# A decoder trunk of two layers on one core: the attention gates as rows made by one product of ones, with bias and partial sums on VectorE

## The chip, the cores and the metric

One core of one Trainium2 chip. The time is the device time of one execution, in microseconds (us); a version's time is the median of its runs.

## The reference, cut to what matters

One sequence of 256 tokens, width 1024, runs through two layers; each is a token mixer and then a mixture of experts (MoE). Layer 0 mixes with stick-breaking attention (16 heads of 64), layer 1 with retention (8 heads, projections 1024 to 6144 and 2048 to 1024). All four sub-layers are modulated by a conditioning vector c:

```python
def adaln_params(c, w, b):
    m = jax.nn.silu(c) @ w + b            # w: 1024 x 3072
    shift, scale, gate = jnp.split(m, 3, axis=-1)
...
for i in range(DEPTH):
    shift, scale, gate = adaln_params(c, ada_w[i, 0], ada_b[i, 0])
    h = x * (1.0 + scale) + shift
    y = stick_breaking_attention(h, ...) if i % 2 == 0 else retention(h, ...)
    x = layer_norm(DEEPNORM_ALPHA * x + (1.0 + gate) * y, ln_g[i, 0], ln_b[i, 0])
    shift, scale, gate = adaln_params(c, ada_w[i, 1], ada_b[i, 1])
    y = grouped_moe(x * (1.0 + scale) + shift, ...)      # 16 experts, top 2
    x = layer_norm(DEEPNORM_ALPHA * x + (1.0 + gate) * y, ln_g[i, 1], ln_b[i, 1])
```

The vector `1 + gate` of the two token mixers is what the change is about.

## The kernel before

The stages follow one another: the stick-breaking attention (called STICK), the MoE of layer 0, retention (RETEN), the MoE of layer 1. In the traces they begin near 40, 180, 445 and 610 us. Within a stage a tile framework orders every engine's instructions by a simulated timeline, so a change in the Python code reorders the work around it. All loads are issued by SyncE (SP) in one queue, 1 MB each.

**Dense blocks.** A weight arrives as fp32. `split_to` makes two parts of it: ScalarE copies a rounded high part (L382), VectorE subtracts to get the low part (L383). `mm3` then runs three matmuls for each product (L403, L404, L405). The token mixers consist mostly of these.

**Stick-breaking attention** works in two halves of 8 heads, `stick_in` and then `stick_attn`. `stick_in` makes q, k and v by dense blocks; v is copied out of PSUM by VectorE (L603). `stick_attn` goes over 4 pairs of heads: the score product z on TensorE (L615, L617), the causal addition on VectorE (L619), three activations on ScalarE (L621 to L623), a combination on VectorE (L624), the suffix sums px on TensorE (L627, L628), their addition on VectorE (L629), an exponential on ScalarE (L630), the product with v on TensorE (L634, L635). z and px have one PSUM buffer each, so the next pair's z waits until VectorE has read the last one, and px likewise.

**The modulation vectors** are computed in the gaps. Sub-layer i (0 attention, 1 its MoE, 2 retention, 3 its MoE) has six chunks j of 512 columns: 0, 1 shift, 2, 3 scale, 4, 5 gate. `plan` puts (i, j) on a list, and each `fill()` between dense blocks takes the next chunk (`ada_part`) and finishes the one before (`rest`). A chunk's weights come in two 1 MB loads. On VectorE it is eight operations, L280 for the first and L282 for seven more, each weight row block times one entry of silu(c) per partition, summed into the tile `e` (128x512). With `on_pe=True` TensorE does it in 16 short matmuls (L277). `rest` then takes the column sums of `e` in four products with `ones` that come out transposed (L292), VectorE adds the bias (L293) and, for scale and gate, 1 (L296). The gate is wanted as a row, equal on all partitions: `gate_row` turns the sums back by four matmuls with the identity for each half (L235) and ScalarE copies each half out (L358). Its tile has one buffer. Chunks (0,4), (0,5) and (2,5) run on VectorE, (2,4) on TensorE.

**Around the change.** The gate of layer 0 is wanted by `out_proj` after the second attention half, that of layer 1 by `ret_out` after the last dense block of retention. `fill` calls stand in `stick_in` after q, after k and after v, and in retention after its dense blocks.

## Time and profile before

| | |
|---|---|
| runs | 904.66, 906.91, 908.5 us; median 906.91 |
| profiled execution | 906.52 us, of which the instructions span 904.8 |
| TensorE busy | 846.6 us (94% of the span) |
| VectorE busy | 499.5 us (55%) |
| ScalarE busy | 274.6 us (30%) |
| GpSimd busy | 21.9 us (2%) |
| DMA | 310.05 MB, mean 343 GB/s |
| mean granted TensorE clock | 0.969 of full speed |

A busy share is an average over four stages with different limits; it doesn't say which engine a given stage waits for. PE stands for TensorE, DVE for VectorE, ACT for ScalarE, POOL for GpSimd, SP for SyncE.

### The profile page before, as it was taken

Reading aid. Unit: us, or ns where it says so; the run is one execution under the profiler, and the core shown is the slowest. Engines: PE = TensorE matmul, PEld = TensorE weight load, DVE = VectorE, ACT = ScalarE, POOL = GpSimd, SP = SyncE. Lnnn points to the kernel's source line nnn. Section 1 sums busy time; section 2 is a strip of 40 time slices with the busy share of each in tenths; the row PEclk is TensorE's granted clock in tenths of the full one; section 3 lists DMA queues with packets and bytes.
Section 4 is the critical chain, followed back from the end, with each engine's and each line's share of the span. In section 5 each row is a group of like instructions: output and inputs, shape, how many; then the busy total and the mean of one; then the engine's idle time right before and its main releaser. Section 6 shows DMA issues by size and latency. Waiting matters only on the chain. (4 is left out here: it accounts for less than half of the span.)

```text
span 904.8 us, 11162 instructions
## 1 busy us (share of the span) xinstructions
PE 846.6 (94%) x4345; PEld 515.9 (57%) x4345; DVE 499.5 (55%) x943; ACT 274.6 (30%) x387; POOL 21.9 (2%) x44
## 2 busy tenths in 40 slices
PE   5799999989969999999799999999999999999993
PEld 1497887764424443434578888888853434334432
DVE  0389999836232235242797899848755423332225
ACT  1347656143101011100534545646341101101101
POOL 0000000000000000000000120011000000000000
PEclk8799999989989999999999999999989999999997
DMA  8999989797999999999679877929749999999971
GB/s 300 386 386 386 365 317 374 265 375 276 420 414 411 416 421 415 416 416 388 210 230 358 310 262 271 332 84 366 291 173 401 416 415 418 415 417 417 418 308 46
DMA packets 90035, 310.05 MB, mean 343 GB/s; under 512 B 5652, under 2 KB 6092, under 8 KB 73588
## 3 DMA queue, kind: packets, MB, share of 16 engines
q1 hardware_dynamic: 89972, 309.23, 88.5%
q8 instruction: 37, 0.61, 0.3%
q14 instruction: 26, 0.21, 0.1%
HBM read 308.17 MB, written 1.05 MB: 342 GB/s over the span
## 5 line engine op out<-in xcount | busy, mean ns | idle before, releaser
L969 PE MATMUL ps<-s,xg 128*64 128x512 f32 x632 | 168.3, 600 | 2.2 <-DVEq L862 1.4
L969 PE MATMUL ps<-w,xg 128*64 128x512 f32 x392 | 111.9, 606 | 6.3 <-PEq L862 6.3
L969 PEld LDWEIGHTS ps<-s,xg 128*64 128x64 f32 x632 | 53.2, 138 | 88.1 <-issue 82.8
L1086 PE MATMUL ps<-w,hidT 128*64 128x512 f32 (+1 forms) x296 | 83.6, 574 | 0.1
L382 ACT ACTIVATE wp<-w 128x1024 fp32r<-128x1024 f32 x57 | 60.1, 1058 | 67.2 <-PE ps L405 60.7
L383 DVE TENSOR_TENSOR wp<-w,wp 128x1024 fp32r<-128x1024 f32 x57 | 69.4, 1220 | 15.1 <-ACT wp L382 14.9
L1019 DVE TENSOR_TENSOR mosg<-mosg,ps 128x512 f32<-128x512 f32 x16 | 11.0, 688 | 118.0 <-PE ps L969 118.0
L1086 PE MATMUL ps<-s,hidT 128*64 128x512 f32 (+1 forms) x248 | 71.8, 568 | 0.0
L969 PEld LDWEIGHTS ps<-w,xg 128*64 128x64 f32 x392 | 35.5, 139 | 63.1 <-issue 60.8
L282 DVE SCALAR_TENSOR_TENSOR s<-w,cact,s 128x512 f32<-128x512 f32 x88 | 65.7, 746 | 0.7
L1051 DVE SCALAR_TENSOR_TENSOR moy<-ps,cs,gate 128x512 f32<-128x512 f32 (+1 forms) x34 | 24.3, 716 | 71.8 <-PE ps L1086 71.8
L382 ACT ACTIVATE moyh<-moy 128x512 fp32r<-128x512 f32 (+1 forms) x34 | 20.6, 605 | 124.2 <-DVE moy L1051 124.2
L404 PE MATMUL ps<-wp,hh 128*128 128x512 f32 (+1 forms) x144 | 56.4, 394 | 0.0
L405 PE MATMUL ps<-wp,hl 128*128 128x512 f32 x144 | 55.5, 390 | 0.0
L454 ACT ACTIVATE xg<-ps,mod 128x256 f32<-128x256 f32 x32 | 17.8, 564 | 122.3 <-PE ps L940 122.3
L403 PE MATMUL ps<-wp,hh 128*128 128x512 f32 (+1 forms) x144 | 53.4, 393 | 1.3 <-ACT wp L382 0.7
L1067 DVE TENSOR_TENSOR res<-res,ps 128x512 f32<-128x512 f32 x48 | 30.3, 683 | 36.7 <-PE ps L1062 36.3
L1086 PEld LDWEIGHTS ps<-w,hidT 128*64 128x64 f32 x296 | 27.1, 136 | 34.0 <-issue 30.9
L1017 ACT ACTIVATE mosg<-ps 128x512 f32<-128x512 f32 x16 | 9.5, 597 | 110.6 <-PE ps L969 110.6
L1086 PEld LDWEIGHTS ps<-s,hidT 128*64 128x64 f32 x248 | 24.7, 137 | 29.9 <-issue 28.8
L403 PE MATMUL ps<-s,wp 128*128 128x256 f32 x128 | 36.6, 288 | 0.6 <-DVE fcol L222 0.6
L405 PE MATMUL ps<-s,wp 128*128 128x256 f32 x128 | 35.2, 285 | 1.1 <-DVE wp L383 1.1
(342 smaller groups left out, 1503.2 us busy)
## 6 DMA issues: line engine op xcount, KB each, us to landing
s<-in_moe_w_up SPq DMA_DIRECT2D x45, 1024.0 KB, 14.5
w<-in_ada_w SPq DMA_DIRECT2D x39, 1024.0 KB, 8.0
w<-in_moe_w_down SPq DMA_DIRECT2D x35, 1024.0 KB, 15.1
s<-in_moe_w_gate SPq DMA_DIRECT2D x34, 1024.0 KB, 13.2
w<-in_moe_w_gate SPq DMA_DIRECT2D x30, 1024.0 KB, 15.3
s<-in_moe_w_down SPq DMA_DIRECT2D x29, 1024.0 KB, 18.2
w<-in_moe_w_up SPq DMA_DIRECT2D x19, 1024.0 KB, 18.5
w<-in_ret_w_in SPq DMA_DIRECT2D x18, 1024.0 KB, 7.1
```

The lines of the kernel that those rows point to most:

```text
L282: V.scalar_tensor_tensor(e, wt[:, kk, :], cact[:, k:k + 1], e, op0=OP.mult, op1=OP.add)
L382: A.activation(hi, src, AF.Copy)
L383: return V.tensor_tensor(lo, src, hi, op=OP.subtract).ins
L403: T.matmul(dst, lh, rh, start=start, stop=False)
L404: T.matmul(dst, lh, rl, start=False, stop=False)
L405: state["mm"] = T.matmul(dst, ll, rh, start=False, stop=stop).ins
L454: return A.activation(dst, src, AF.Identity, scale=sc[:, k:k + 1], bias=sh[:, k:k + 1]).ins
L969: state["mm"] = T.matmul(o[64 * u:64 * u + 64, :], xg[:, k, at:at + CAP], ts[u][kk], start=(k == 0), stop=(k == NK - 1)).ins
L1019: V.tensor_tensor(sgt, sgt, pu, op=OP.mult)
L1051: V.scalar_tensor_tensor(y, py, cs, gate[:, c0:c0 + n], op0=OP.mult, op1=OP.mult)
L1067: V.tensor_tensor(r, r, sos[b], op=OP.add)
L1086: state["mm"] = T.matmul(py[64 * u:64 * u + 64, :], hidT[:, f, u * CAP:(u + 1) * CAP], ts[h][u][:, i, c0:c0 + n], start=(f == 0), stop=(f ...
```

## The change

The chunks (0,4), (0,5), (2,4) and (2,5), the gates of the two token mixers, become `direct`. A zeroed tile `brow` (128x512, one buffer, kept for the whole program) takes the chunk's bias row in its first partition by a DMA of 2 KB; the first of the eight VectorE operations adds `brow` instead of only multiplying (L287 of the changed kernel); the finishing step `row` is one product of the 128x128 tile `ones` with `e`, which sums over the partitions and leaves the sum on all of them at once, and one ScalarE copy that adds 1 and writes half of the gate row. `rest` and `gate_row` go for these chunks. Chunk (2,4) moves from TensorE to VectorE. The MoE gates keep `rest` and `gate_row`.

```diff
+    sums, gates = {}, {}
+    brow = keep([P, 512], "brow")
+    G.memset(brow, 0.0)
...
+        direct = i % 2 == 0 and j >= 4
+        if direct:
+            if i not in gates:
+                gates[i] = tmp([P, D], "gate", 1)
+            SY.dma_start(brow[0:1, :], ada_b[l, s, j * 512:(j + 1) * 512].rearrange("(o d) -> o d", o=1))
...
+                elif k == 0 and direct:
+                    V.scalar_tensor_tensor(e, wt[:, kk, :], cact[:, 0:1], brow, op0=OP.mult, op1=OP.add)
...
+        def row():
+            pt = ps((P, 512), "po" if state["name"] == "RETEN" else "ps")
+            T.matmul(pt, ones, e, start=True, stop=True)
+            A.activation(gates[i][:, (j - 4) * 512:(j - 3) * 512], pt, AF.Copy, bias=1.0)
...
-        return rest
+        return row if direct else rest
...
-        gate = gate_row(2)
+        gate = gates[2]
...
-    gate = gate_row(0)
+    gate = gates[0]
...
-    plan(2, range(4, 5), on_pe=True)
-    plan(2, range(5, 6))
+    plan(2, range(4, 6))
```

Lines of the old code stand 7 to 15 lines further down in the changed kernel: L282 is L291 there, L383 L398, L403 to L405 L418 to L420, L603 L618, L615 L630, L619 L634, L624 L639, L627 and L628 L642 and L643, L629 L644. New are L278 (DMA of the bias row), L287 (first operation of a direct chunk), L301 (product with ones), L302 (copy of the row).

TensorE, first attention half, before: px of a pair of heads, then dense products (names `ps`, with weights `wp`), then z of the next pair, then the next dense block.

```order
L627 MATMUL px_620<-s_135 128x384
L628 MATMUL px_620<-s_135 128x128
L627 MATMUL px_620<-s_135 128x384
L628 MATMUL px_620<-s_135 128x128
L404 MATMUL ps_520<-wp_571,s_200 128x512
...
L615 MATMUL pz_658<-s_251,s_252 128x256 x2
L617 MATMUL pz_658<-s_251,s_252 128x128 x2
L403 MATMUL ps_707<-s_200,wp_711 128x256
L404 MATMUL ps_707<-s_201,wp_711 128x256
```

The same place in the changed kernel:

```order
L420 MATMUL ps_522<-wp_572,s_203 128x512
L630 MATMUL pz_655<-s_253,s_254 128x256 x2
L632 MATMUL pz_655<-s_253,s_254 128x128 x2
L642 MATMUL px_617<-s_137 128x384
L643 MATMUL px_617<-s_137 128x128
L642 MATMUL px_617<-s_137 128x384
L643 MATMUL px_617<-s_137 128x128
L630 MATMUL pz_679<-s_253,s_254 128x256 x2
L632 MATMUL pz_679<-s_253,s_254 128x128 x2
L642 MATMUL px_641<-s_82,s_137 128x384
L643 MATMUL px_641<-s_82,s_137 128x128
L642 MATMUL px_641<-s_82,s_137 128x384
```

Four attention steps stand back to back, with no dense product between them. Behind them follow the products with v, the row product L301 of chunk (0,5) and only then the dense block that stood between them.

VectorE at the same place, before. L282 are the operations of the modulation chunks, L383 splits of dense weights, L603 the copies of v.

```order
L383 TENSOR_TENSOR wp_711<-lo_709,wp_711 128x1024
L629 TENSOR_TENSOR s_207<-s_207,px_620 128x768
L280 TENSOR_SCALAR s_82<-w_831,cact 128x512
L603 COPY s_252<-ps_520 128x512
L282 SCALAR_TENSOR_TENSOR s_82<-w_831,cact,s_82 128x512
L603 COPY s_252<-ps_521 128x512
L282 SCALAR_TENSOR_TENSOR s_82<-w_831,cact,s_82 128x512
L619 TENSOR_TENSOR s_207<-pz_658,s_135 128x768
L383 TENSOR_TENSOR wp_738<-lo_709,wp_738 128x1024
L282 SCALAR_TENSOR_TENSOR s_82<-w_831,cact,s_82 128x512
L624 SCALAR_TENSOR_TENSOR s_82<-s_82 128x768
```

The changed kernel:

```order
L398 TENSOR_TENSOR wp_708<-lo_706,wp_708 128x1024
L618 COPY s_254<-ps_521 128x512
L291 SCALAR_TENSOR_TENSOR s_82<-lo_599,cact,s_82 128x512
L618 COPY s_254<-ps_522 128x512
L291 SCALAR_TENSOR_TENSOR s_137<-w_515,cact,s_137 128x512
L398 TENSOR_TENSOR wp_735<-lo_706,wp_735 128x1024
L634 TENSOR_TENSOR s_209<-pz_655,s_137 128x768
L639 SCALAR_TENSOR_TENSOR s_82<-s_82 128x768
L291 SCALAR_TENSOR_TENSOR s_82<-lo_599,cact,s_82 128x512
L644 TENSOR_TENSOR s_209<-s_209,px_617 128x768
L291 SCALAR_TENSOR_TENSOR s_137<-w_515,cact,s_137 128x512
L634 TENSOR_TENSOR s_137<-pz_679,s_137 128x768
```

The third causal addition (L619, now L634) stands behind the split and both copies in either; the addition of the suffix sums (L629, now L644), which stood ahead of the copies, now stands behind the third causal addition and the combination L639.

VectorE in the first dense blocks of retention, before. L645 to L651 are the rotary embedding.

```order
L383 TENSOR_TENSOR s_3343<-w_3341,s_3343 128x1024
L383 TENSOR_TENSOR wp_3358<-w_3341,wp_3358 128x1024
L383 TENSOR_TENSOR wp_3387<-w_3385,wp_3387 128x1024
L383 TENSOR_TENSOR s_3402<-w_3385,s_3402 128x1024
L645 TENSOR_TENSOR s_3373<-ps_3307,trig 128x512
L649 TENSOR_TENSOR s_3374<-ps_3307,trig 128x4x64 x2
L645 TENSOR_TENSOR s_3373<-ps_3308,trig 128x512
L649 TENSOR_TENSOR s_3374<-ps_3308,trig 128x4x64 x2
L651 TENSOR_TENSOR s_3373<-s_3373,s_3374 128x512
L383 TENSOR_TENSOR wp_3419<-w_3417,wp_3419 128x1024
```

The changed kernel, with chunk (2,4) now on VectorE:

```order
L398 TENSOR_TENSOR s_3327<-w_3325,s_3327 128x1024
L398 TENSOR_TENSOR wp_3342<-w_3325,wp_3342 128x1024
L287 SCALAR_TENSOR_TENSOR s_3257<-w_3544,cact,brow 128x512
L398 TENSOR_TENSOR wp_3371<-w_3369,wp_3371 128x1024
L291 SCALAR_TENSOR_TENSOR s_3257<-w_3544,cact,s_3257 128x512
L398 TENSOR_TENSOR s_3386<-w_3369,s_3386 128x1024
L291 SCALAR_TENSOR_TENSOR s_3257<-w_3544,cact,s_3257 128x512
L660 TENSOR_TENSOR s_3357<-ps_3291,trig 128x512
L664 TENSOR_TENSOR s_3358<-ps_3291,trig 128x4x64 x2
L660 TENSOR_TENSOR s_3357<-ps_3292,trig 128x512
L664 TENSOR_TENSOR s_3358<-ps_3292,trig 128x4x64 x2
L291 SCALAR_TENSOR_TENSOR s_3257<-w_3544,cact,s_3257 128x512
```

Operations of chunk (2,4) stand between the splits (L398) from the fourth one on; before, the first operation of a gate chunk stood behind the place shown.

## Rows read from the trace of the kernel before

**Rows 1.** The chain of work that ended last, followed back from the last instruction: shares of the span by engine.

```profile
PE 17%; DVE 2%; ACT 0%; issue 0%; DVEq 0%; ACTq 0%
```

**Rows 2.** Five stretches of 20 us, one in each stage (two in retention): length, then busy time (and count) of PE, PE's weight loads, DVE, ACT, POOL; then the granted clock, the DMA share, GB/s.

```profile
140.00:160.00 20.00, 19.80 (x112) 14.96 (x111) 18.48 (x29) 12.62 (x19) 0.00 (x0) 1.00 0.99 377
200.00:220.00 20.00, 18.45 (x99) 8.60 (x99) 12.51 (x25) 6.33 (x9) 0.00 (x0) 1.00 0.58 217
460.00:480.00 20.00, 20.00 (x102) 15.23 (x101) 19.16 (x29) 8.70 (x11) 0.00 (x0) 1.00 0.81 275
560.00:580.00 20.00, 20.00 (x105) 16.95 (x104) 19.96 (x37) 12.24 (x20) 0.00 (x0) 1.00 0.98 345
700.00:720.00 20.00, 20.00 (x102) 8.71 (x98) 7.20 (x13) 2.28 (x4) 0.00 (x0) 1.00 1.01 415
```

**Rows 3.** ScalarE's longest wait from 440 to 540 us: what waited, what for; us in total, times, longest.

```profile
ACT wp L382 <- PE ps L405: 28.7, 17, 5.1
```

**Rows 4.** TensorE in order of time, for prices (here and in all groups below: start, duration, engine, line, operation, tiles, form, count): the four transposing products of a chunk (fp32, two instructions each) and the product behind them, half of `gate_row` (four products, likewise) and the product behind it, two pairs of 256 columns in fp32, the 16 products of chunk (2,4) and the product behind them.

```profile
177.12 0.95 PE L292 MATMUL ps<-con,s 128*128 128x2 f32 x8
178.01 0.64 PE L277 MATMUL ps<-lo,cact 128*32 128x512 f32 x4
...
143.54 1.16 PE L235 MATMUL ps<-con,sums 128*128 128x128 f32 x8
144.45 0.47 PE L403 MATMUL ps<-wp,oh 128*128 128x512 f32 x1
...
607.23 0.59 PE L690 MATMUL pz<-s,s 128*128 128x256 f32 x2
607.66 0.59 PE L691 MATMUL pz<-s,s 128*128 128x256 f32 x2
...
471.05 1.92 PE L277 MATMUL ps<-w,cact 128*32 128x512 f32 x16
472.90 0.50 PE L403 MATMUL ps<-wp,hh 128*128 128x512 f32 x1
473.24 0.40 PE L404 MATMUL ps<-wp,hh 128*128 128x512 f32 x1
```

**Rows 5.** TensorE in the first attention half: px of a pair and the product behind it, z of the next pair and the product behind it, a product with v and the product behind it.

```profile
78.41 0.81 PE L627 MATMUL px<-s 128*128 128x384 f32 x2
...
80.06 0.48 PE L404 MATMUL ps<-wp,s 128*128 128x512 f32 x1
...
82.53 0.70 PE L615 MATMUL pz<-s,s 64*128 64x256 f32 x4
...
83.38 0.38 PE L403 MATMUL ps<-s,wp 128*128 128x256 f32 x1
...
99.35 0.66 PE L634 MATMUL po<-s,s 128*64 128x256 f32 x4
...
100.16 0.39 PE L403 MATMUL ps<-s,wp 128*128 128x256 f32 x1
```

**Rows 6.** VectorE in the first attention half, three places.

```profile
70.37 0.95 DVE L619 TENSOR_TENSOR s<-pz,s 128x768 f32<-128x768 f32 x1
71.24 0.74 DVE L282 SCALAR_TENSOR_TENSOR s<-w,cact,s 128x512 f32<-128x512 f32 x1
71.90 1.22 DVE L383 TENSOR_TENSOR wp<-w,wp 128x1024 fp32r<-128x1024 f32 x1
73.03 0.15 DVE L293 TENSOR_TENSOR sums<-ps,col 128x4 f32<-128x4 f32 x1
73.11 0.74 DVE L282 SCALAR_TENSOR_TENSOR s<-lo,cact,s 128x512 f32<-128x512 f32 x1
...
83.01 0.48 DVE L280 TENSOR_SCALAR s<-w,cact 128x512 f32<-128x512 f32 x1
83.41 0.68 DVE L603 COPY s<-ps 128x512 f32<-128x512 f32 x1
84.01 0.74 DVE L282 SCALAR_TENSOR_TENSOR s<-w,cact,s 128x512 f32<-128x512 f32 x1
...
93.12 0.95 DVE L624 SCALAR_TENSOR_TENSOR s<-s 128x768 f32<-128x768 f32 x1
93.98 0.74 DVE L282 SCALAR_TENSOR_TENSOR s<-w,cact,s 128x512 f32<-128x512 f32 x1
```

**Rows 7.** TensorE in the output projection of the attention; in square brackets the idle time before the instruction and what ended it.

```profile
168.56 0.50 PE L404 MATMUL ps<-wp,oh 128*128 128x512 f32 x1 [0.94 <-DVE wp L383]
```

**Rows 8.** VectorE in retention, splits of dense weights and one operation of a modulation chunk.

```profile
452.24 1.23 DVE L383 TENSOR_TENSOR s<-w,s 128x1024 fp32r<-128x1024 f32 x1 [1.67 <-ACT s L382]
...
470.05 1.22 DVE L383 TENSOR_TENSOR wp<-w,wp 128x1024 fp32r<-128x1024 f32 x1
471.19 0.75 DVE L282 SCALAR_TENSOR_TENSOR s<-w,cact,s 128x512 f32<-128x512 f32 x1
...
476.84 1.23 DVE L383 TENSOR_TENSOR wp<-lo,wp 128x1024 fp32r<-128x1024 f32 x1 [0.77 <-ACT wp L382]
...
482.98 1.23 DVE L383 TENSOR_TENSOR wp<-lo,wp 128x1024 fp32r<-128x1024 f32 x1 [0.81 <-ACT wp L382]
485.69 1.23 DVE L383 TENSOR_TENSOR wp<-w,wp 128x1024 fp32r<-128x1024 f32 x1 [1.49 <-ACT wp L382]
...
489.62 1.23 DVE L383 TENSOR_TENSOR s<-w,s 128x1024 fp32r<-128x1024 f32 x1 [2.31 <-ACT s L382]
```

**Rows 9.** SyncE's issue of the load that stands behind the second bias row in the changed kernel; and loads by destination and source with the median us from issue to landing.

```profile
55.19 2.50 SPq L165 DMA_DIRECT2D s<-in_sb_w_in  x1
...
lo<-in_ada_w SPq DMA_DIRECT2D x6, 1024.0 KB, 10.6
...
w<-in_sb_w_in SPq DMA_DIRECT2D x8, 1024.0 KB, 14.5
...
w<-in_moe_w_up SPq DMA_DIRECT2D x19, 1024.0 KB, 18.5
```

**Rows 10.** ScalarE in the first attention half: the load of an activation table and the activation behind it.

```profile
72.48 1.28 ACT L622 ACT_TABLE_LOAD   x1
73.77 0.84 ACT L622 ACTIVATE s<-s 128x768 f32<-128x768 f32 x1
```

More of the change, by code (lines that the diff above doesn't have):

```diff
@@ L261, in rotary_tables @@
             V.tensor_scalar(trig[:, 1, b, :], trig[:, 2, b, :], -1.0, None, op0=OP.mult)
-    sums = {}
+    sums, gates = {}, {}
+    brow = keep([P, 512], "brow")
+    G.memset(brow, 0.0)
     def ada_part(i, j, on_pe):
```

## The prediction

> **What bounds the kernel now.** I read the chain of waits first, and it answers little here: it follows the end of the program back through the last MoE only (17% of the span on TensorE) [rows 1]. So I went to the stretches by stage [rows 2]. The reader is to see two kinds. In the attention of layer 0 and in retention TensorE is busy 19.80 and 20.00 of 20 us, and VectorE stands right beside it, at 18.48, 19.16 and 19.96 of 20. In the MoE of layer 1 the DMA moves 415 GB/s at a share of 1.01, with VectorE at 7.20. Between the two lies the start of the first MoE: there the DMA share is 0.58, so the loads wait for buffers that TensorE has to free, and a shift of the attention's end is passed on. The waits of ScalarE say the same for retention: its splits waited 28.7 us for products (L405) that had to free their buffers, 17 times [rows 3]. Both attention stages run at TensorE's pace, with a VectorE that has almost nothing to spare; the granted clock is 1.00 in all five stretches, so the sum needs no term for it.
>
> I therefore count TensorE's work in the two stages, and look for each place where the new order makes it wait for VectorE. A microsecond there is a microsecond at the end. The sum is made against the profiled execution, 906.52 us, 0.4 below the median of the runs shown (906.91).
>
> **TensorE's work in the attention of layer 0.** Durations are taken from one start to the next, since products overlap. The four transposing products of a chunk take 0.95 as their row gives it (0.89 from start to start; I keep the row's), half of `gate_row` 144.45 − 143.54 = 0.91 [rows 4]. The new row product, 512 columns in fp32, has no row of its own; the nearest are two fp32 pairs of 256 columns, 607.66 − 607.23 = 0.43 each, so 0.86. Its bounds are 0.43 (one pass of the two would do) and 0.95 (no better than what it replaces); 0.86 is the same form and length. Two chunks: −2 x 0.95 − 2 x 0.91 + 2 x 0.86 = **−2.0 us**.
>
> **The order in the first half.** Before, the four attention steps stand between dense products. After, z, px, z, px, the products with v and the row product of chunk (0,5) stand back to back behind the last dense product. z and px have one PSUM buffer each, so every step of this run needs VectorE to have read the one before. Without any wait the next dense block would begin at 83.38 (as before) − 0.95 (products that go) + 1.65 (px, 80.06 − 78.41) + 0.85 (z, 83.38 − 82.53) + 0.81 (product with v, 100.16 − 99.35) + 0.86 = 86.6 [rows 5].
>
> Against this stands what VectorE has to do first. Its steps, from start to start: causal addition 0.87, modulation product 0.66, split 1.13, copy of v 0.60, combination 0.86 [rows 6]. In the new order, from the first causal addition at 70.37 to the end of the third (which frees z for the fourth pair) there stand 3 x 0.87 + 9 x 0.66 + 4 x 1.13 + 0.86 + 2 x 0.60 = 15.13 us, so the fourth z begins at 85.5 at the earliest. The second px needs VectorE's first suffix addition: 0.86 + 0.66 + 0.86 later, 87.9. The row product needs the last two products of its chunk, behind the next causal addition: 0.66 + 0.87 + 2 x 0.66 later, 90.7. With 0.86 for itself the dense block begins at 91.6 in place of 86.6: **+5.0 us**. Bounds: nothing, if VectorE's work ahead of 70.37 comes earlier by as much; 5.0 is taken because VectorE is 90% busy here and nothing is taken off it.
>
> **The order in the second half** is like it: the third z, px, the fourth z, px and the products with v, without the dense products that stood between the two px. From the end of the dense products VectorE has a copy, a product, a copy, the combination, a split and a causal addition ahead of the fourth z: 0.60 + 0.66 + 0.60 + 0.86 + 1.13 + 0.87, and twice the 0.08 of a small addition (73.11 − 73.03) [rows 6], 4.9 us. TensorE has 0.85 + 1.65 = 2.5. That is +2.4; the suffix addition then ends at 4.9 + 0.66 + 0.86 = 6.4 where TensorE is at 5.75: +0.65. Together **+3.0 us**.
>
> In the output projection TensorE now waits 0.94 for a split [rows 7]; a TensorE that comes later by more than that finds it done: **−0.9**. The stage: −2.0 + 5.0 + 3.0 − 0.9 = **+5.1 us**.
>
> **Retention.** TensorE is rid of the 16 products of chunk (2,4), 472.90 − 471.05 = 1.85, of two times four transposing products (−1.9) and of `gate_row` (−1.8), and gets two row products (+1.7): **−3.85 us**. VectorE gets eight products, 8 x 0.66 = 5.3. Six more than before stand ahead of the split at 470.05, 4.0 us; VectorE was idle for 1.67 before the split at 452.24 and fills that, so this split ends 2.3 later, at 473.6. TensorE wanted it at 473.24 and wants it at 471.4 without the 16 products [rows 4, 8]: **+2.2 us**. Behind it VectorE has 0.77, 0.81, 1.49 and 2.31 idle ahead of its next splits [rows 8], which take up the rest. The stage: −3.85 + 2.2 = **−1.65 us**.
>
> **What I cost at nothing.** Clearing `brow` is GpSimd's, idle in all stretches [rows 2]. The bias in the first product makes it a operation with two inputs, 0.66 in place of 0.40 (83.41 − 83.01) [rows 6], in three chunks, counted at 0.66 above; against that go L293 and L296 of four chunks. The copy of the row replaces that of `gate_row` one to one on ScalarE. `brow` has one buffer: each next bias row waits on SP's queue for the first product of the chunk before, and with it every load behind it; by the order on VectorE that product stands a whole chunk earlier, so I add nothing, and price the other case below. ScalarE loads its activation tables six times in place of three in the first half, since two pairs of heads now alternate; 3 x 1.28 [rows 10] lie beside a VectorE chain that is longer.
>
> **Sum:** +5.1 − 1.65 = +3.45, so 906.5 + 3.5 = **910.0 us**.
>
> **Rivals.**
> *A, the bunched order costs nothing* (faster). The products alone: −2.0 − 3.85 = −5.85, 900.7 us. For it: VectorE's products of modulation chunks are due to nobody soon, and if they slip behind, the causal additions come earlier. Against it: within an engine the order is fixed, and the products stand ahead of them.
> *B, half of the stalls* (5.1 of 10.2): 910.0 − 5.1 = 904.9. For it: the chain from 70.37 has nine products in it, and a start of that chain 2 to 3 us earlier is enough.
> *C, VectorE bounds retention's start* (slower). If the splits' idle times [rows 8] are no reserve, because each is ScalarE waiting for TensorE and slips with it, all 5.3 us of chunk (2,4) come on the path in place of 2.2: +3.1, 913.1. It decides when the idle ahead of 452.24 doesn't fill; TensorE at 20.00 of 20 [rows 2] speaks against it.
> *D, the second bias row is late* (slower). VectorE wants it at 71.24, right behind the causal addition [rows 6]; it can't be issued before about 55.2, where the next load's issue stands [rows 9], so it decides from 16.0 us of landing. Loads land in 10.6 and 14.5 us at the median here, in 18.5 at the worst of the three groups [rows 9]: by the last, 71.24 becomes 73.7, +2.5, 912.5. The row is 2 KB, but stands in one queue behind loads of 1 MB. The Trainium skill ("DMA: Bandwidth & Descriptors", on the anatomy of one DMA) has, for a transfer that GpSimd issues, a fixed cost of about 2 us and then the bytes; by that estimate the row would land near 57 and never be late. No row here shows a transfer of this size behind such a queue.
> *E, each table load holds ScalarE longer than its row* (slower). If a load held up the engine for as long again, the four ahead of the second combination would cost 4 x 1.28 = 5.1 more, 915.1 at most. In the row the next activation starts at 73.77, right at the end of the load that began at 72.48 [rows 10], which speaks against it. The Trainium skill ("ScalarE: Activation LUTs", on what ACT_TABLE_LOAD costs) names, beside about 1.28 us for the load, a drain of about 1.38 us; this trace shows the first and not the second.
>
> **How the numbers follow.** A measurement of this kernel tells 0.5%, about 4.5 us, from no change: under 902.4 is faster, over 911.4 slower. Forecast 0.42; its own range is 907 to 913 (each stall within a third), of which 0.27 lies in the same band and 0.15 above. A 0.25: 0.22 faster, 0.03 same. B 0.16, same. C 0.09, D 0.05, E 0.03, slower. That makes 0.22 faster, 0.46 same, 0.32 slower. The range reaches down to A's products alone and up to C and D, 900.0 to 914.5; left out are E and the tails of A and C, under 0.2. The forecast and B and A differ in one thing, how much TensorE waits in the first attention half and at its end.
>
> **What would show it.** In the changed profile: a TensorE idle time ahead of the fourth z, the second px and the row product of chunk (0,5) in the first half, released by VectorE, 5 us in all; 3 us at the end of the second half; the output projection's 0.94 gone; in retention an idle of some 2 us ahead of the products of the eleventh split, 16 short products fewer; the first MoE starting 5 us later, the second 3.5 us later. L301 with a start to start of 0.86. Wrong would be the forecast if the dense block of v's half begins near 86.6 with no idle ahead (A), if TensorE in retention is idle by 5 us or more (C), or if VectorE is idle ahead of L287 near 71 us (D).

## The result and the profile after

The changed kernel takes 919.02 us (median of 4 runs, 918.94 to 922.22) against 907.7 for the kernel before (4 runs, 904.66 to 908.5): ratio 1.0149, interval 1.0121 to 1.0177. It is slower by 1.5%, outside the range given, and by three times what was forecast.

The first lines of the page after; work has not grown:

```profile
span 917.4 us, 11022 instructions
## 1 busy us (share of the span) xinstructions
PE 846.5 (92%) x4273; PEld 515.9 (56%) x4273; DVE 505.7 (55%) x943; ACT 277.7 (30%) x389; POOL 23.0 (3%) x45
```

TensorE's busy time is that of before (846.6) though it has 72 matmul instructions fewer: a product at half the clock counts as busy for longer. The totals therefore say little, and the stages have to be read one by one. I cut each trace at five TensorE instructions: the first z of the attention, the first product of the first MoE (on `oneh`), the first transposing product of the norm that begins retention, the first product of the second MoE, the last product. Us between them:

| kernel | first z at | attention, layer 0 | first MoE | retention | second MoE |
|---|---|---|---|---|---|
| before | 68.1 | 134.0 | 236.6 | 226.7 | 228.2 |
| after | 69.5 | 142.1 | 232.7 | 228.8 | 233.3 |
| e1_l0 | 70.3 | 146.6 | 232.6 | 225.1 | 233.3 |
| e2_l2 | 69.2 | 135.5 | 236.4 | 224.5 | 232.5 |
| e3_pool | 69.9 | 146.6 | 232.5 | 228.1 | 233.5 |
| e4_split | 70.9 | 137.4 | 232.2 | 230.7 | 232.8 |
| e5_apad | 68.9 | 146.7 | 232.5 | 239.7 | 229.3 |
| e6_bpad | 68.1 | 150.1 | 235.1 | 226.5 | 226.3 |
| e7_l2pad | 69.2 | 151.6 | 235.2 | 236.7 | 227.1 |
| e8_pe24 | 70.5 | 142.7 | 232.5 | 225.1 | 232.6 |
| e9_bq | 70.4 | 135.5 | 231.9 | 225.9 | 226.4 |
| e10_l2q | 70.9 | 135.5 | 231.5 | 225.6 | 225.9 |
| e11_aq | 68.5 | 144.6 | 232.6 | 228.1 | 225.5 |
| e12_s24q | 69.1 | 135.8 | 232.8 | 224.9 | 232.1 |
| e13_warm | 69.3 | 138.7 | 238.5 | 225.4 | 233.5 |

After against before: +1.4 ahead of the first z, +8.1 in the attention, −3.9 in the first MoE, +2.1 in retention, +5.1 in the second MoE; 12.8, where the spans differ by 12.6. The sum forecast +3.45; of the 9.3 that it misses, 3.7 are retention's, 3.0 the attention's, 1.4 come ahead of the first z and 1.2 from the MoEs. The first column goes with the time at which the granted clock rises at the program's start (at 39.0 us in the kernel before, at 46.0 in e9_bq). The attention of unchanged code takes 134.0 or 135.5, and all of that difference lies at its end: up to the first product with `part` (L292, after L307; the column sums of a later modulation chunk, behind the output projection) it takes 112.6 us in each of before, e2_l2, e9_bq and e10_l2q, and the rest, 21.4 or 22.9, goes with the granted clock there (0.84 in the kernel before, over 180.7 to 202.1). Retention of unchanged code takes 225.1 to 226.7. Where nothing finer is given, less than 2 us is not read from one trace.

**The attention.** TensorE after, at the run of attention steps that [rows 5] showed apart; in square brackets the idle time ahead of an instruction and what ended it:

```profile
83.05 0.81 PE L642 MATMUL px<-s 128*128 128x384 f32 x2
83.70 0.38 PE L643 MATMUL px<-s 128*128 128x128 f32 x2
87.65 1.22 PE L630 MATMUL pz<-s,s 64*128 64x256 f32 x4 [3.56 <-DVE s L634]
88.66 0.64 PE L632 MATMUL pz<-s,s 64*128 64x128 f32 x4
90.04 1.65 PE L642 MATMUL px<-s,s 128*128 128x384 f32 x2 [0.74 <-DVE s L644]
91.48 0.63 PE L643 MATMUL px<-s,s 128*128 128x128 f32 x2
91.91 1.38 PE L642 MATMUL px<-s,s 128*128 128x384 f32 x2
...
94.24 1.13 PE L301 MATMUL ps<-s,con 128*128 128x512 f32 x2
94.81 0.68 PE L418 MATMUL ps<-s,wp 128*128 128x256 f32 x1
```

The waits are those that were forecast, for the steps that were named: 3.56 for the causal addition of the third pair, 0.74 for the first suffix addition. What follows is new: z's first part takes 1.22 where it took 0.70 [rows 5], px 1.65 where it took 0.81. The stretches of 4 us (columns as in [rows 2]) say why:

```profile
84.00:88.00 4.00, 0.44 (x3) 0.35 (x4) 4.00 (x6) 3.33 (x3) 0.00 (x0) 0.78 1.04 386
88.00:92.00 4.00, 3.26 (x13) 2.18 (x12) 4.00 (x6) 0.84 (x1) 0.00 (x0) 0.50 1.05 376
92.00:96.00 4.00, 4.00 (x22) 2.56 (x22) 2.31 (x4) 1.63 (x3) 0.00 (x0) 0.87 1.00 350
96.00:100.00 4.00, 4.00 (x35) 3.56 (x34) 2.12 (x4) 3.97 (x6) 0.00 (x0) 1.00 0.45 168
```

While TensorE waited the granted clock fell to 0.50 (1.2 GHz), and it came back some 7 us later. What that cost is less than what the steps lost by it, since VectorE was late too. Its last products for the row product:

```profile
91.44 1.52 DVE L291 SCALAR_TENSOR_TENSOR s<-w,cact,s 128x512 f32<-128x512 f32 x2
```

At the full clock the second px would have taken 1.65 from 90.04 and the product with v 0.81, to 92.5; the row product would have had to wait for VectorE until 92.96, in place of beginning at 94.24. So the fall cost about 1.3 us here. The second half has the same again, at the fourth z and the px behind it:

```profile
147.32 0.94 PE L630 MATMUL pz<-s,s 64*128 64x256 f32 x4 [3.12 <-DVE s L634]
...
148.84 1.65 PE L642 MATMUL px<-s 128*128 128x384 f32 x2 [0.16 <-DVE s L644]
```

**The MoEs** differ too, though the change doesn't touch their code. The first product behind the jump over the spill block (code for tokens that don't fit, skipped here; `tc.If` in `spill`) in the first and the second MoE, before:

```profile
267.02 1.98 PE L969 MATMUL ps<-w,xg 128*64 128x512 f32 x4 [6.32 <-PEq L862]
...
725.47 1.12 PE L969 MATMUL ps<-s,xg 128*64 128x512 f32 x2 [1.40 <-DVEq L862]
```

After, two rows for the first jump and one for the second:

```profile
271.77 1.08 PE L984 MATMUL ps<-w,xg 128*64 128x512 f32 x4 [1.51 <-DVEq L877]
...
276.44 1.08 PE L984 MATMUL ps<-w,xg 128*64 128x512 f32 x4 [1.87 <-issue]
...
737.95 1.12 PE L984 MATMUL ps<-s,xg 128*64 128x512 f32 x2 [6.21 <-PEq L877]
```

The long wait has moved from the first MoE to the second. Its releaser is TensorE's own sequencer (PEq) at the jump. The MoE that has it is 3.9 and 5.1 us longer than the same MoE in the other kernel. The waits alone differ by 2.9 (6.32 against 1.51 and 1.87) and 4.8; in the first MoE the clock adds to it, for the four product instructions behind the long wait take 1.98 in place of 1.08.

**Retention** has the two early waits that were forecast, and a late one that was not:

```profile
478.25 0.50 PE L418 MATMUL ps<-wp,hh 128*128 128x512 f32 x1 [0.69 <-ACT wp L397]
...
480.68 0.50 PE L419 MATMUL ps<-wp,hh 128*128 128x512 f32 x1 [1.24 <-DVE wp L398]
...
553.20 0.73 PE L418 MATMUL ps<-s,hh 128*128 128x512 f32 x2 [2.18 <-ACT s L397]
```

ScalarE ahead of the last one:

```profile
550.50 1.70 ACT L721 ACTIVATE s<-s,rs 128x256 f32<-128x256 f32 x4 [5.08 <-POOL rs L714]
552.11 1.04 ACT L397 ACTIVATE s<-lo 128x1024 fp32r<-128x1024 f32 x1
```

A group of normalising activations (L721) stands ahead of a split on ScalarE's queue and waits 5.08 us for GpSimd; the split comes after it, and TensorE waits for the split.

### The profile page after: what moved, and what is told of

The parts are those of the page before. It is cut to its first block, busy times and chain, and to the rows that moved or that the text cites. A ratio compares the mean times of both kernels' runs of the same rounds, so it can differ in the third digit from the quotient of the medians.

```text
span 917.4 us, 11022 instructions
## 1 busy us (share of the span) xinstructions
PE 846.5 (92%) x4273; PEld 515.9 (56%) x4273; DVE 505.7 (55%) x943; ACT 277.7 (30%) x389; POOL 23.0 (3%) x45
## 5 line engine op out<-in xcount | busy, mean ns | idle before, releaser
L398 DVE TENSOR_TENSOR wp<-w,wp 128x1024 fp32r<-128x1024 f32 x57 | 69.3, 1219 | 20.2 <-ACT wp L397 20.1
L291 DVE SCALAR_TENSOR_TENSOR s<-w,cact,s 128x512 f32<-128x512 f32 x95 | 70.6, 745 | 0.9
L420 PE MATMUL ps<-wp,hl 128*128 128x512 f32 x144 | 56.3, 396 | 0.0
L418 PE MATMUL ps<-wp,hh 128*128 128x512 f32 (+1 forms) x144 | 53.8, 400 | 1.6 <-ACT wp L397 1.4
L418 PE MATMUL ps<-s,wp 128*128 128x256 f32 x128 | 37.7, 298 | 0.6 <-DVE fcol L222 0.6
L419 PE MATMUL ps<-s,wp 128*128 128x256 f32 x128 | 36.4, 288 | 0.0
```

Source lines behind the costliest of these rows:

```text
L291: V.scalar_tensor_tensor(e, wt[:, kk, :], cact[:, k:k + 1], e, op0=OP.mult, op1=OP.add)
L398: return V.tensor_tensor(lo, src, hi, op=OP.subtract).ins
L418: T.matmul(dst, lh, rh, start=start, stop=False)
L419: T.matmul(dst, lh, rl, start=False, stop=False)
L420: state["mm"] = T.matmul(dst, ll, rh, start=False, stop=stop).ins
```

## The experiments

Ratios are against the kernel before on the same chip, with intervals. The kernel before took 904.1 to 905.2 us there. Theory O (order), V, S, W, D, L (jump), C (clock) are as the expectations name them; the letters of the prediction's rivals are others.

**e1_l0: direct gates in layer 0 alone.**

```diff
-        direct = i % 2 == 0 and j >= 4
+        direct = i == 0 and j >= 4
...
-        gate = gates[2]
+        gate = gate_row(2)
...
-    plan(2, range(4, 6))
+    plan(2, range(4, 5), on_pe=True)
+    plan(2, range(5, 6))
```

> Direct gates in layer 0 alone; retention is the code of before. In the changed kernel the first product of the first MoE came 9.5 us later than before, the first of the second MoE another 0.2 us on top of what the first MoE had taken back. Theory O (the bunched order of the first layer's attention, its waits and the lower clock behind them): the order of all engines there is that of the changed kernel, so the same two waits of about 3.5 and 3 us and the same 9 to 10 us at the end of that stage; in total 912 to 917, retention as long as before (226.7 us from its first transposing product to the first product of the second MoE). Rival V (the loss is retention's, by the eight products more on VectorE): 906 to 909.

919.58 us, ratio 1.0167 (1.0119 to 1.0216): as slow as the whole change, and over O's range. Attention 146.6, retention 225.1. Rival V falls: layer 0 carries the loss. The attention is longer than the 9 to 10 us expected (12.6), and the second MoE is 5.1 longer though nothing of layer 1 is changed.

**e2_l2: direct gates in layer 1 alone.**

```diff
-        direct = i % 2 == 0 and j >= 4
+        direct = i == 2 and j >= 4
...
-    gate = gates[0]
+    gate = gate_row(0)
```

> Direct gates in layer 1 alone, chunk (2,4) on VectorE; the first layer is the code of before. Theory O: the first MoE begins near 202 as before, retention takes 2 us more than before (228.8), in total 908 to 911. Rival V: the whole loss is here, 916 to 919.

911.13 us, 1.0068 (1.0046 to 1.0091), just over O's range, but for another reason: retention is not longer, it is 224.5, 2.2 shorter than before (e1_l0, whose retention is the code of before, is 1.6 shorter too), with the early waits (0.70 and 1.23) and without the late one. What makes it slower is the second MoE, 232.5, with 6.10 at its jump; the first has 6.45.

**e3_pool: the bias rows in GpSimd's queue.**

```diff
-            SY.dma_start(brow[0:1, :], ...)
+            G.dma_start(brow[0:1, :], ...)
```

> The whole change, with the four bias rows fetched by GpSimd's queue in place of SP's; the order on TensorE, VectorE and ScalarE is that of the changed kernel. Theory O: same waits, 917 to 921. Rival S (the second bias row, waiting in SP's queue, holds back the loads behind it, which were issued at 74.1 in place of 71.3): the loads come at their old times and most of the loss goes, 908 to 912.

922.82 us, 1.0195 (1.0152 to 1.0239), just over O's range. The load that SP issued at 74.06 in the changed kernel goes out at 74.45 here. SP's queue was not what held it: rival S falls. The order and the waits of the attention are the same (3.56, 0.74, 3.10), yet it takes 146.6 in place of 142.1. The clock differs. The stretches of 5 us from 145, the changed kernel:

```profile
145.00:150.00 5.00, 2.52 (x10) 1.80 (x11) 4.97 (x11) 1.08 (x2) 0.00 (x0) 0.77 0.96 378
150.00:155.00 5.00, 5.00 (x29) 3.77 (x28) 4.89 (x8) 2.02 (x3) 0.00 (x0) 0.89 1.04 391
155.00:160.00 5.00, 5.00 (x27) 3.70 (x26) 4.96 (x10) 4.89 (x6) 0.00 (x0) 1.00 1.03 399
```

and here:

```profile
145.00:150.00 5.00, 1.51 (x9) 1.17 (x10) 5.00 (x9) 0.50 (x1) 0.00 (x0) 0.87 1.00 390
150.00:155.00 5.00, 5.00 (x18) 2.87 (x17) 4.86 (x9) 1.62 (x3) 0.00 (x0) 0.50 0.96 333
155.00:160.00 5.00, 5.00 (x16) 4.24 (x17) 4.86 (x9) 3.27 (x5) 0.00 (x0) 0.50 1.01 394
160.00:165.00 5.00, 5.00 (x19) 3.77 (x19) 1.92 (x3) 2.12 (x3) 0.00 (x0) 0.77 0.85 314
```

The same wait is followed once by a short fall of the clock and once by a long one: (1 − clock) times the length adds to 1.7 us in the first and 6.8 in the second. The difference, 5.1, is about that of the stages, 4.5. The other runs with this order fall into the same two groups: behind the same wait the loss is 6.8 in e1_l0 and e5_apad (attention 146.6 and 146.7) and 1.7 in e8_pe24 and e11_aq (142.7 and 144.6, of which 1.5 lie behind the output projection).

**e4_split: both bias rows of a layer in one tile, no row waits for the other chunk.**

```diff
-            SY.dma_start(brow[0:1, :], ...)
+            if j == 4:
+                for n in range(2):
+                    SY.dma_start(brow[64 * n:64 * n + 1, :], ada_b[l, s, 2048 + 512 * n:2560 + 512 * n]...)
...
-                    V.scalar_tensor_tensor(e, wt[:, kk, :], cact[:, 0:1], brow, ...)
+                    h, g = (slice(0, 64), slice(64, P)) if j == 4 else (slice(64, P), slice(0, 64))
+                    V.scalar_tensor_tensor(e[h], wt[h, kk, :], cact[h, 0:1], brow[h], ...)
+                    V.tensor_scalar(e[g], wt[g, kk, :], cact[g, 0:1], None, op0=OP.mult)
```

> The whole change, but both bias rows of a layer lie in one tile (partitions 0 and 64) and come before the layer's first gate chunk; each chunk's first operation becomes two of 64 partitions, one with the bias and one without. No chunk waits for the other's row, and in the order the z and px steps of both attention halves have dense products between them again. Theory O (what bunched the order is the wait of chunk (0,5) for its bias row): no wait over 1.5 us on TensorE between 60 and 180 us, the first MoE begins at 200 to 203, in total 904 to 910. Rival W (the row products and VectorE's added work cost the time in themselves): nothing changes, 917 to 921.

915.52 us, 1.0106 (1.0057 to 1.0155), between the two forecasts: O's sum left out the second MoE (232.8) and retention's late wait, which is there again (2.17; 230.7). The attention is 137.4, 4.7 under the changed kernel's. In the first half the two waits are 0.74 and 0.84 and the clock stays at 1.00; in the second one of 2.83 is left, so O's limit of 1.5 us does not hold there:

```profile
89.00 0.70 PE L634 MATMUL pz<-s,s 64*128 64x256 f32 x4 [0.74 <-DVE s L638]
...
148.86 0.66 PE L653 MATMUL po<-s,s 128*64 128x256 f32 x4 [2.83 <-DVE s L638]
```

In the order, the products of chunk (0,5) now stand ahead of the first attention half as before; in the changed kernel they stand inside it, behind the wait for the second bias row. With the wait for the second row taken away the first half's run goes, so that wait is its cause. In the second half 3.12 with it stand against 2.83 without; the cause of that wait was not separated.

**e5_apad: 36 tiny products ahead of the second MoE's routing.**

```diff
+    def pad(n, after=None):
...
+                for _ in range(n):
+                    T.matmul(t, ident, ones[:, 0:2], start=True, stop=True)
...
             warm(2, state["row"])
+            pad((0, 36)[l], state["row"])
```

> The changed kernel with 36 tiny products (128x2, output unused) on TensorE ahead of the second MoE's routing, where TensorE waits anyway. They make TensorE's instruction count ahead of the skipped spill block of the second MoE the same as in the kernel before (2645 products by the order, 2609 in the changed one). Theory L (the wait of TensorE at that jump, 1.4 us before and 6.2 after, hangs on where the code behind the jump stands in the instruction stream): the wait at the jump of the second MoE falls to about 1.4, that MoE takes 228 to 229 us in place of 233.3 from its first product, the time falls by 3 to 5 us against the changed kernel without them. Rival D (the wait is one on loads or on VectorE that came from the change's later start): 6.2 and the time stay.

926.02 us, 1.0216 (1.0188 to 1.0243). The time is a miss: the products stand ahead of the routing on TensorE, which waits for them (retention, as cut here, 239.7). The wait at the jump is as L said, 1.40 in place of 6.21:

```profile
748.86 1.12 PE L992 MATMUL ps<-s,xg 128*64 128x512 f32 x2 [1.40 <-DVEq L884]
```

**e6_bpad: the kernel before, with 50 and 14 such products; e7_l2pad: layer 1 alone, with 50 and 36.**

```diff
+            pad((50, 14)[l], state["row"])     # (50, 36) in e7_l2pad
```

> The kernel before with 50 tiny products ahead of the first MoE's routing and 14 ahead of the second's. Theory L with a period of 64 such products: the count at the first jump, 948, is that of the changed kernel plus 64, so its wait falls from 6.3 to two short ones (1.5 and 1.8); at the second it is that of before plus 64, so 1.4 as before. The first MoE takes 232 to 233 us in place of 236.6; in total 2 to 5 us faster than before. Rival D: as before within 1 us (slower by what the products take). If the period is another one, the waits differ from both.

922.6 us, 1.0196 (1.0164 to 1.0229): again the padding's own price, 16 us ahead of the first MoE. The waits at the jumps: 1.51 and 1.83 at the first, 1.40 at the second, as L with its period says.

> Direct gates in layer 1 alone, with 50 and 36 tiny products in the two places, which give both jumps the counts of the run before this one (948 and 2709). Theory L: the first MoE 232 to 233, the second 228 to 229, retention 224 to 225 as without the products; in total 3 to 7 us faster than the kernel before. Rival D: as direct gates in layer 1 alone, 4 to 8 us slower than before.

931.96 us, 1.0282 (1.0249 to 1.0315); 1.52 and 1.56, then 1.40. Waits as said, time missed for the same reason.

**e8_pe24: the whole change, but chunk (2,4) on TensorE.**

```diff
-        direct = i % 2 == 0 and j >= 4
+        direct = i % 2 == 0 and j >= 4 and not on_pe
...
+        A.activation(gate[:, 0:512], row_ps(sums[2][:, 16:20]), AF.Copy)
...
-    plan(2, range(4, 6))
+    plan(2, range(4, 5), on_pe=True)
+    plan(2, range(5, 6))
```

> The whole change, but chunk (2,4) stays on TensorE with its transposing products and its half of the gate row through the identity; the first layer's order is that of the changed kernel. Theory O: the two waits of the early retention (0.69 and 1.24 us) go, since they come from chunk (2,4)'s products on VectorE ahead of the splits, while TensorE gets 1.85 + 0.95 + 0.91 - 0.86 = 2.85 us of work back: retention 228 to 230, in total 918 to 922. Rival V (VectorE's added work in retention is what costs): retention 224 to 226, 914 to 917.

916.41 us, 1.0128 (1.0097 to 1.0159). Retention is 225.1: the two early waits go, as O said, but so does the late one, and stage and total come out where V put them. So chunk (2,4) on VectorE costs the 3.7 us between 228.8 and 225.1 in the whole change. In e2_l2 and e10_l2q the same chunk on VectorE costs nothing (224.5 and 225.6), and there the order came out without the late wait.

**e9_bq, e10_l2q, e11_aq: the padding where TensorE waits anyway**, products of 2x2 at the program's start and ahead of retention's norm; 50 and 14 in the kernel before, 50 and 36 in layer 1 alone, 0 and 36 in the changed kernel.

```diff
+    def pad(n):
+        t = ps([2, 2])
+        for _ in range(n):
+            T.matmul(t, part, part, start=True, stop=True)
+    pad(50)
...
     phase("RETEN", "second")
+    with urgent():
+        pad(14)
```

> The kernel before with tiny products of 2x2 in places where TensorE waits anyway: 50 at the program's start and 14 ahead of the norm that begins retention. The order of VectorE, ScalarE and SP is that of before. Theory L (the wait at each jump hangs on where it stands in the instruction stream, with a period of 64 products): first jump 1.5 and 1.8 us in place of 6.3, second 1.4 as before; without the price of the earlier padding, the first MoE 232 to 233 us, in total 3 to 5 us faster than before. Rival: the waits fall, but the loads of the MoE set its time, and it stays at 236.6; same time as before.

902.75 us, 0.9975 (0.996 to 0.9991): faster than the kernel before by 1.5 us, where 3 to 5 were expected; the attention's 135.5 and a first z at 70.4 take some of the 4.7 us that the first MoE (231.9) gains. The rival, that loads set the MoE's time, falls.

> Direct gates in layer 1 alone, with 50 tiny products at the start and 36 ahead of the norm. Theory L: both jumps short, the first MoE 232 to 233, the second 228 to 229, retention 224 to 226; 895 to 900, faster than the kernel before by 4 to 9 us. Rival: 904 to 908.

900.48 us, 0.994 (0.9922 to 0.9959): faster than both kernels, the best of all, and just over the range expected. Its jumps:

```profile
266.56 0.65 PE L991 MATMUL ps<-w,xg 128*64 128x512 f32 x2 [1.51 <-DVEq L884]
...
270.87 1.08 PE L991 MATMUL ps<-w,xg 128*64 128x512 f32 x4 [1.51 <-issue]
...
723.62 0.65 PE L991 MATMUL ps<-s,xg 128*64 128x512 f32 x2 [1.40 <-DVEq L884]
```

> The changed kernel with 36 tiny products ahead of the norm of retention. Theory L: the second jump 1.4 in place of 6.2, the second MoE 228 to 229 in place of 233.3, so 4 to 5 us less than the changed kernel (919.0), 913 to 916. What is then left against the kernel before is the first layer's attention (8 to 12 us) and retention (2).

912.57 us, 1.0087 (1.0055 to 1.0118), just under the range. The second MoE is 225.5, its jump 1.40. With 36 products the count of matmul instructions on the page is 4345, that of before.

**e12_s24q: the edits of e4_split and e8_pe24 together, no padding.**

> The whole change without the wait for the second bias row (both rows in one tile, partitions 0 and 64), chunk (2,4) on TensorE, no padding. Theory O: first layer's attention 3 to 4 us over before, as in the run without that wait; retention 224 to 226 as with (2,4) on TensorE; first MoE 232 and second 232.5 by the jumps: 905 to 909. Rival V (VectorE's operations in the first layer cost 8 us or more whatever the order): 913 to 917.

909.15 us, 1.0058 (1.0033 to 1.0083): just over O's range, far under V's. Attention 135.8 (up to the first product with `part` 116.1, as in e4_split, 3.5 over before), retention 224.9; the second MoE keeps its long jump (232.1).

**e13_warm: four unused products in each of the two long waits of the attention.**

```diff
+            if m == (0, 0)[half]:
+                t = ps(tag="po")
+                with urgent(), tc.issue_after(pxm):
+                    for _ in range(4):
+                        state['wm'] = T.matmul(t, ident, con[:, 0:512], start=True, stop=True).ins
...
+            with tc.issue_after(state["wm"]) if m == 3 else nullcontext():
```

The first hunk adds the products behind a px in each half, the second holds back the z of pair m == 3 until they have been issued.

> The changed kernel with four unused products (128x512, fp32, 3.4 us at the full clock) on TensorE in each of its two long waits in the first layer's attention, between the px of one pair of heads and the z of the next. VectorE's order up to there is that of the changed kernel, so the waits themselves stay, but TensorE is busy in them. Theory C (the clock that falls behind each wait costs 3.4 us in the first half and 1.7 to 7 in the second, on top of the waits): granted clock 1.00 from 80 to 100 us and at the second place; the dense block behind the first run of attention steps begins near 91 to 92 in place of 94.8 (with the start of the first z at 69.5), and from the first z to the first product of the first MoE it takes 137 to 139 us in place of 142.1. Rival (the clock costs nothing there, since TensorE waits for VectorE whatever its clock): 142 to 147.

918.83 us, 1.0159 (1.0109 to 1.0208). The attention takes 138.7, 3.4 under the changed kernel's, in the range of C. But only 1.5 of this lie where products were added, up to the first product with `part` (119.3 against 120.7); the other 2.0 lie behind it, where the granted clock was 1.00 in this run and 0.84 in the changed kernel. And the two places differ. In the second the clock stays at 1.00 from 145 to 165. In the first the wait is filled, and the clock falls all the same, behind the next wait:

```profile
83.72 3.60 PE L649 MATMUL po<-con 128*128 128x512 f32 x8
87.44 0.70 PE L631 MATMUL pz<-s,s 64*128 64x256 f32 x4
...
89.83 1.10 PE L643 MATMUL px<-s,s 128*128 128x384 f32 x2 [1.47 <-DVE s L650]
...
94.78 1.13 PE L301 MATMUL ps<-s,con 128*128 128x512 f32 x2 [0.51 <-DVE s L291]
95.34 0.68 PE L418 MATMUL ps<-s,wp 128*128 128x256 f32 x1
```

z is at its full speed (0.70), but the px behind it is slow again (1.10 for 0.81), and the dense block begins at 95.34, no earlier than in the changed kernel (94.81). The first half therefore doesn't test C, since the clock fell in it all the same. In the second half the order behind the place differs from the changed kernel's too, so that the 1.5 us are the clock's and the order's together; the two groups of runs under e3_pool are the cleaner evidence. The first MoE is 238.5, with 6.39 at the jump: eight products more have moved it back to the long wait.

**The jump, over all runs.** By the order, so many products stand ahead of it, and so long was the wait (first jump, then second):

| products ahead of the first | wait | products ahead of the second | wait |
|---|---|---|---|
| 884 (after, e1, e3, e4, e5, e8, e11, e12) | 1.51 to 1.57 (in most with another of 1.75 to 1.87 behind) | 2609 (after, e3, e4) | 6.19 to 6.21 |
| 948 (e6, e7, e9, e10) | 1.51 and 1.52 (1.51 to 1.83 behind) | 2617, 2623, 2624, 2631 (e13, e2, e8 and e12, e1) | 6.10 to 6.28 |
| 892 (e13) | 6.39 | 2645 (before, e5, e11) | 1.40 |
| 898 (before, e2) | 6.32 and 6.45 | 2709 (e6, e7, e9, e10) | 1.40 |

Equal counts have equal waits, whatever the kernel, and 64 products more make no difference. With an equal wait a MoE is not yet equally long: at 1.40 the second one takes from 225.5 (e11_aq, mean granted clock 1.00) to 229.3 (e5_apad, 0.98). Each of these products is four instructions on TensorE (on the page matmuls and weight loads are equal in number, and the row [rows 4] has eight matmuls for four products; the 16 matmuls of chunk (2,4) are eight products likewise), so 64 are 256 instructions. The Trainium skill ("Runtime: NRT & Kernel Launch", Instruction fetch mechanics) says that an engine's instructions are fetched in blocks of 256, and that a taken jump to a target outside the two blocks that it holds has to wait for the target's block. A period of 256 instructions agrees with the runs, though a half or a quarter of it would fit their counts too. That the 6.2 us are such a fetch is a reading by the page; what the runs show is that the wait goes with the position.

## Why the prediction was wrong, step by step

- *The waits in the attention.* Forecast +5.0 and +3.0; measured 3.56 + 0.74 = 4.30 and 3.12 + 0.16 = 3.28, together 7.6 against 8.0. The mechanism was right, and so were four of the five places. The fifth, the row product in the first half, did not wait: at half the clock TensorE came to it later than VectorE, so there the clock's cost stands in the wait's place.
- *"The granted clock is 1.00 in all five stretches, so the sum needs no term for it."* **This step failed.** The stretches were those of a TensorE that did not wait; the forecast itself put waits of 3 to 5 us there. The clock fell to 0.50 behind each: about 1.3 us in the first half, by the working above, and up to 1.7 in the second, 6.8 in e3_pool's; with the long fall the same order takes 146.6. The stretch from the first z to the first product with `part`, before and after (columns as in [rows 2]):

```profile
68.12:180.71 112.59, 110.25 (x698) 88.94 (x697) 102.06 (x169) 63.34 (x78) 1.11 (x2) 1.00 0.93 341
69.51:190.25 120.74, 110.74 (x676) 88.48 (x675) 107.58 (x174) 66.61 (x80) 1.11 (x2) 0.96 0.86 311
```

TensorE's idle time (length less its busy time) goes from 2.3 to 10.0, by 7.7 where 8.0 − 0.9 = 7.1 was forecast. Its work ran at half the clock for long enough to lose 3.9: 5.1 in the rows of 4 and 5 us above, less 1.2 in which it waited. The stretch is 8.1 longer, all that the stage lost, so −3.5 is left for the work itself.
- *TensorE's work in the attention,* −2.0 and the −0.9 at the output projection: the wait of [rows 7] is gone, but waits of 0.15, 0.49 and 0.43 for ScalarE's splits stand there in its place, so the −0.9 came to nothing. The row product takes the 0.86 forecast where its own start and the next one's can be read (492.60 to 493.46 in retention). The −2.0 is not seen apart in any run; the −3.5 above holds it, and what the rest is was not separated.
- *Retention's early wait,* forecast +2.2: 0.69 + 1.24 = 1.93. Right. *"Idle ahead of its next splits, which take up the rest"* failed in the changed kernel: the late wait of 2.18 is one of ScalarE's order, which was not looked at, and the clock falls behind it as well (mean 0.79 over 552 to 560). In the kernel with that stage changed alone (e2_l2) it is absent, and the stage is 2.2 shorter, where −1.65 was forecast; but against e1_l0, whose retention is the code of before at as good a clock (0.99), it is 0.6 shorter, so the −1.65 was not reached and the 2.2 are in the main the clock's.
- *A term that was missing:* the MoEs were taken to pass the shift on. The jumps gave back 3.9 in the first and took 5.1 in the second. Nothing in the forecast looked at code that the change doesn't touch. A row of the kernel before showed the 6.32; it was not asked what sets it.
- *The rivals.* D (bias row late) and C (retention's start) did not happen: VectorE had no gap ahead of the first operation with the second bias row (72.63), and the early waits of retention stayed at 1.9. A and B did not happen either. None of the rivals had the clock or the jump.

The cleanest sum is between kernels of one session whose jumps have the same short waits: e11_aq is 9.8 us over e9_bq (912.57 and 902.75; 8.9 by the profiled spans), 9.1 in the attention and 2.2 in retention, less 2.1 in the rest, 1.9 of it ahead of the first z. With layer 1 alone (e10_l2q) the change gains 2.3 (900.48 against 902.75), although the stage table puts only 0.3 of that in retention and the rest within its scatter. So direct gates cost nothing in layer 1 where the late wait is absent, and fail in layer 0, where VectorE was busy 102 of 112.6 us already and a bias row with one buffer moved eight of its operations into the attention. Without the wait for that row (e4_split, e12_s24q) 3.5 us of the 8.1 are left.

Open: what leaves the 2.83 us in the second half of e4_split and e12_s24q, and what decides between a short and a long fall of the clock behind the same wait.

## What to carry to other kernels

A wait that an order puts on TensorE is not paid by its length alone: ask what the clock does behind it, and whether whoever was late is late again anyway. A gap of some us at a jump in code that a change does not touch can still move with the change, since it hangs on the count of instructions ahead of it; compare the untouched stages first, and set the count with a few cheap products where the engine waits anyway, before judging a change of 1%. A helper tile with one buffer is a dependence between the two jobs that use it, and a scheduler will move the second job, not only its copy.

## What the runs showed of the hardware

- The wait of TensorE behind a skipped block of code is 1.4 to 1.6 us or 6.1 to 6.5, by its position in the instruction stream; 64 fp32 products more leave it as it is. Before against after it is worth 4 to 5 us for each MoE, 0.5% of the kernel.
- Behind a wait of 3.1 us the granted clock fell to 0.50, for a loss of 1.7 us in three traces and 6.8 in three others, with the same order. In e13_warm it fell (0.66 over 90 to 95) where a wait of 3.6 us had been filled and one of 1.47 was left.
- 50 products of 128x128 by 128x2 took 16.3 us ahead of the routing in e6_bpad, at a granted clock of 0.62 and 0.50 from 205 on, although TensorE counted as busy for 5.00 of every 5 us there up to 215; with tiles of 2x2 at the program's start the same number cost nothing that stands out of the scatter of the first column.
